# S5's preparation on S5's own pages, layer 0's column tiles in a new order, retention in nine turns

## The chip, the core and the metric

One core of one Trainium2 chip runs the whole program. The metric is the device time in microseconds; the median of three runs of the kernel before is 1762.29 us (1761.71 to 1763.96).

## What is computed

Two layers of a hybrid network on 640 tokens (128 of a context pass, 512 of a denoising step), 1024 features each, all in 32-bit floats. Per layer, cut to what matters here:

```python
mod = silu(cond) @ mod_w + mod_b                 # six vectors sh1, sc1, g1, sh2, sc2, g2
h = rmsnorm(x, norm1_w) * (1 + sc1) + sh1
proj = h @ w_in                                  # 1024 -> 2568 columns
pa, pb, pc, pd = split(proj)                     # SSD, retention, S5, LRU
ya = ssd_mixer(pa);  yb = retention_mixer(pb)
yc = s5_mixer(pc);   yd = lru_mixer(pd)
x = x + g1 * (concat(ya, yb, yc, yd) @ w_out)
h = rmsnorm(x, norm2_w) * (1 + sc2) + sh2
x = x + g2 * conv_ffn(h)
```

SSD and retention are chunked scans with 128-token chunks, S5 is a complex diagonal scan, LRU a real one; each runs in both directions. S5 needs tables (powers and angles of its decay, products of its input and output matrices) that depend on the parameters alone; the kernel computes them too.

## The kernel before

Features lie on partitions, the 640 tokens along the free dimension, in two halves of 320. A matrix product in 32 bits is made of three products in a rounded format: weights and activations are split into a high and a low part (`hi`, `lo`, `hhi`, `hlo`), and `mm3` multiplies high by high, high by low and low by high. `wsplit` (line 186) fetches 512 columns of weights into `raw`, rounds them on ScalarE into `hi`, and subtracts on GpSimd and VectorE in turn into `lo`. `col_tile` (line 214) makes one column tile: 128 output features from all 1024 inputs, 48 matmuls of 320 columns, into two of the three PSUM banks of tag `mm`.

Working memory is given out in pages of 128 x 648 floats under tags: A, B and C have 12 each, Ya, Yb, Yc and Yd two each, H 16 (line 121). A tile takes a free page of its tag, and a helper adds an order between first writes: of two tiles of one tag, the one that comes first in the program is first written first. So a tile waits for a free page and for all earlier tiles of its tag to have been begun. Banks are given out in the same way (line 124: `mm` three, `b` two, `a`, `c` and `mod` one each). The order on each engine is laid down when the program is built, by a planner that takes the program's order as priority and its own estimates of durations; on the chip every engine works through its list in order. DMAs are all issued from the SP queue.

In the layer (line 1360) each mixer is a generator, and the string `ORDER` (line 44) says whose next turn is emitted. The mixers' column tiles are made in their turns: two for S5, two for LRU, two for LRU's gate (`gb`), one narrow one and four for SSD, two for its gate (`z`), and for retention two each for queries and keys (q0, k0, q1, k1), two for the gate (g0, g1) and the values (v). The turn "a0" or "a1" is the attention over one pair of heads. After every turn in layer 0 two rounds of the modulation product are emitted (`filler`, line 321): a round fetches two pages of `mod_w` (`mraw`, on the two pages of Yd) and makes 8 small matmuls; `drain` emits what is left, ahead of the first turn that needs Yd for retention's output.

In layer 0, S5's preparation (`s5_prep`, line 592) is emitted just behind S5's column tiles. Its tiles are under three tags, set by `ST = 'AAC'`: powers, angle tables and small matrices on A (12 pages, those LRU and retention use as well), the four large turns on C (those of SSD). Its PSUM tiles are on the one bank `c`. In layer 1 the preparation is made during the feed-forward part of layer 0, and all on C. S5's scans, and the eight tiles of `x` themselves, are on B: `x` is freed when it has been normalized, and fetched again (`load_x`, line 177) behind S5's last tile; the residual of the output projection needs it.

The output projection is in two halves: LRU and S5 (8 tiles), then SSD and retention. Its inputs are split onto pages (`yhi`, `ylo`; `parts`, line 1407); the first half takes the pages of tag H, on which the normalized activations were.

Of the kernel before, what the change touches and what calls it, by code (L numbers as in the profile page):

```python
# [12 lines left out]
AF = mybir.ActivationFunctionType  # L13
# [16 lines left out]
NF = 22  # L30
TB = 81
SK = 2
PB = "c"
EXTRA = ''
TBA = 1
PCP = 1
# [2 lines left out]
TSR = 1  # L39
LB = 1  # L40
FPS = 2
ST = 'AAC'
MR = 'C'

ORDER = ("s5 gb lru lru gb ssd ssd z lru ssd z ret ret ssd ret ssd ret ret ret ret",
         "s5 ssd gb lru ssd lru gb z lru ssd z ret ssd ret ret ssd ret ret ret ret")
RAWS = 5
SPLITS = 5

# [26 lines left out]
def hybrid_kernel(ctx: ExitStack, tc: tile.TileContext, I, O, dbg=None):  # L76
# [3 lines left out]
    sec = ["start"]  # L80
# [45 lines left out]
    def page(tag, dt=F32, name="pg"):  # L126
        t = pgp.tile([P, PGB if tag == "B" else PGW], dt, tag=tag, name=name, bufs=PAGES[tag])
        fresh[t.tensor.name] = tag
        return t

    def paged(tag, shape, name, dt=F32):
        n = int(np.prod(shape))
        t = page(tag, dt, name)[:, :n]
        if len(shape) == 1:
            return t
        names = "abcd"[:len(shape)]
        return t.rearrange(f"p ({' '.join(names)}) -> p {' '.join(names)}", **dict(zip(names[1:], shape[1:])))

    def bank(tag):
        t = psp.tile([P, 512], F32, tag=tag, name=tag, bufs=BANKS[tag])  # L140
        fresh[t.tensor.name] = tag
        return t
# [43 lines left out]
    def wsplit(ap, n, cut=512, le=None, tag=None):  # L186

        out = []
        for c0 in range(0, n, cut):
            w = min(cut, n - c0)  # L190
            raw = wp.tile([P, 512], F32, tag="raw", name="raw", bufs=RAWS)
            SP.dma_start(raw[:, :w], ap[:, c0:c0 + w])
            if tag:
                hi, lo = page(tag, F32R, "whi")[:, :512], page(tag, F32R, "wlo")[:, :512]
            else:
                hi = wp.tile([P, 512], F32R, tag="hi", name="hi", bufs=SPLITS)
                lo = wp.tile([P, 512], F32R, tag="lo", name="lo", bufs=SPLITS)
            A.copy(hi[:, :w], raw[:, :w])
            lo_i[0] += 1
            (le or lo_eng[lo_i[0] % len(lo_eng)]).tensor_tensor(lo[:, :w], raw[:, :w], r2f(hi[:, :w]), op=ALU.subtract)  # L200
            out.append((c0, c0 + w, hi, lo))
        return out
# [289 lines left out]
    M_, A_, S_ = ALU.mult, ALU.add, ALU.subtract  # L492
# [99 lines left out]
    def s5_prep(l):  # L592

        wb, wc, tb, zz = s5d[l]
        p1, p2, p3 = "CCC" if l else ST

        def keep(name, shape):
            return smp.tile([P] + shape, F32, tag=f"k_{name}", name=name)
# [65 lines left out]
            G.tensor_copy(s5x0[l][DH[d], :, :, d].rearrange("p g i -> p i g"), x0[DH[d]])  # L664
        yield


        ek = [u8]
        for k in range(1, 6):
# [4 lines left out]
        for q in range(2):  # L674
            o = 8 * q
# [43 lines left out]
             [bb[:, i] for i in range(2)], [bt[:, i] for i in range(2)])  # L719
        ncq = paged(p2, [16, 16], "ncq")  # L720
        V.tensor_scalar(ncq, cq[:, 1], -1.0, None, op0=M_)
        cm = [paged(p2, [16, 32], f"cm{i}") for i in range(2)]
        for i, c in enumerate((cq[:, 0], ncq)):
            G.memset(cm[i], 0.0)
            for d in range(2):
# [65 lines left out]
    def s5_mixer(l, hh, y, steps):  # L791
# [132 lines left out]
        for i in range(2):  # L924
            tp = page("B", name="glut")
            for h in range(2):
                o, n = HALF[h]
                t = tp[:, o:o + n]
                for vg in (1, 0):
                    ps = bank("b")  # L930
                    for k in range(2):
                        m = 256 * vg + 128 * i
                        T.matmul(ps[:, :n], gw[k][:, m:m + 128], yt[k][:, o:o + n], start=k == 0, stop=k == 1)
                    if vg:
                        A.activation(t, ps[:, :n], AF.Tanh, scale=0.5)
                    else:
                        V.scalar_tensor_tensor(t, t, 1.0, ps[:, :n], op0=A_, op1=M_)
                G.tensor_scalar(y[i][:, o:o + n], t, 0.5, None, op0=M_)


    def lru_mixer(l, hh, y):
# [296 lines left out]
    def ret_mixer(l, hh, y):  # L1238
# [9 lines left out]
        def rotated(u):  # L1248
            pss = col_tile(wsplit(I["w_in"][l, u], 1024), hh)
            q = page("A", name="rq")  # L1250
            evac(pss, q)
            sw = page("A", name="rsw")
            V.stream_shuffle(sw[:, :512], q[:, 128:640], swap)
            V.tensor_tensor(sw[:, :512], sw[:, :512], sinp[:, :512], op=M_)
            G.tensor_tensor(q[:, 128:640], q[:, 128:640], cosp[:, :512], op=M_)
            V.tensor_tensor(q[:, 128:640], q[:, 128:640], sw[:, :512], op=A_)
            return q
# [35 lines left out]
                            T.matmul(out, S[d][:, k - 1], qe[d][:, k - 1], start=False, stop=d == 1)  # L1293
                A.copy(y[t][:, 128 * k0:128 * (k0 + n)], ps[:, 0:128 * n])

        yield
        q = rotated(12)
        yield
        kx = rotated(13)
        yield  # L1300
        units = wsplit(I["w_in"][l, 14], 1024) + wsplit(I["w_in"][l, 15], 1024)
        vk = [paged("B", [5, 128], "rv") for _ in range(2)]
        for c0 in (0, 2, 4):
            n = min(2, 5 - c0)
            ps = bank("b")
            old = sec[0]
            sec[0] = old + "*"
            for c in range(n):
                for k in range(8):
                    hi, lo = units[k // 2][2:]  # L1310
                    w = slice((k % 2) * 256, (k % 2) * 256 + 256)

                    mh, ml = [v[:, 128 * (c0 + c):128 * (c0 + c) + 128] for v in hh[k]]
                    o = ps[:, 256 * c:256 * c + 256]
                    T.matmul(o, mh, hi[:, w], start=k == 0, stop=False)
                    T.matmul(o, mh, lo[:, w], start=False, stop=False)
                    T.matmul(o, ml, hi[:, w], start=False, stop=k == 7)
            sec[0] = old
            for i in range(2):
                A.copy(vk[i][:, c0:c0 + n], ps[:, 0:256 * n].rearrange("p (c w) -> p c w", w=256)[:, :, 128 * i:128 * i + 128])  # L1320
        attend(0, q, kx)
        yield
        q = rotated(16)
        yield
        kx = rotated(17)
        gg = [page("A", name="rg") for _ in range(2)]
        gt = gates(l, hh, (18, 19), gg, None if TSR else AF.Silu)
        next(gt)
        for _ in range(2):
            yield  # L1330
            next(gt)
        attend(1, q, kx)
        SP.dma_start(O["st_ret"][l], so)

        nw = smp.tile([P, 2], F32, tag="rnw", name="rnw")
# [24 lines left out]
    def layer(l, norm):  # L1360
# [6 lines left out]
            for h in HO:  # L1367
                norm.apply(l, 0, h, hh, ks)
        normed = hold[1]
        ys = {n: [page(tag, name="y" + n) for _ in range(2)] for n, tag in (("lru", "Ya"), ("ssd", "Yb"), ("s5", "Yc"))}  # L1370
        ys["ret"] = []
        gens = {"s5": s5_mixer(l, hh, ys["s5"], steps), "lru": lru_mixer(l, hh, ys["lru"]), "ssd": ssd_mixer(l, hh, ys["ssd"]),
                "ret": ret_mixer(l, hh, ys["ret"]), "gb": gates(l, hh, (2, 3), ys["lru"], AF.Gelu_apprx_tanh),
                "z": gates(l, hh, (9, 11), ys["ssd"], None if TSZ else AF.Silu)}
# [10 lines left out]
                hold[0] = None  # L1385
        order = ORDER[l].split()
        for i, n in enumerate(order):
            if n == "ret" and "ret" not in order[:i]:
                if l == 0:
                    drain()  # L1390
                ys["ret"] += [page("Yd", name="yret") for _ in range(2)]
                step(n + str(l), gens[n])
            step(n + str(l), gens[n])
            if i == 0 and l == 0:
                load_x(0)
            if l == 0 and i >= 1:
                filler(FPS)
# [346 lines left out]
```

## Time and profile before

| | us |
|---|---|
| median of three runs | 1762.29 |
| the profiled execution | 1760.15 |
| its span, first to last instruction | 1758.30 |
| TensorE matmul busy | 1659.0 |
| VectorE busy | 1042.9 |
| ScalarE busy | 712.0 |
| GpSimd busy | 466.2 |

The profile is of one execution. Engines are named PE (TensorE), PEld (its weight loads, which overlap), DVE (VectorE), ACT (ScalarE), POOL (GpSimd) and SP (the queue that issues DMAs). Almost every instruction is recorded under line 92, a helper, so that groups are told apart by the names of their tiles: `out<-in`. Matmuls overlap, so that the busy time of a group can be longer than the stretch it ran in.

### The profile page before, as it was taken

How to read it: one execution, taken by the hardware profiler on the slowest of the kernel's cores; microseconds unless marked ns; L12 is line 12 of the kernel's file. 1: busy time of each engine (PE TensorE's matmuls, PEld its weight loads, DVE VectorE, ACT ScalarE, POOL GpSimd, SP SyncE). 2: the span in 40 equal slices, each digit the busy share in tenths (PEclk: the TensorE clock that was granted, in tenths of full speed). 3: DMA queues.
4: the chain of work that ended last, by engine and by line, in shares of the span. 5: the costliest groups of instructions: out<-in, count | busy, mean ns of one | idle time of the engine just before them, and what ended most of it. 6: DMA issues, size and time to landing. Idle time of an engine off the chain costs nothing.

```text
span 1758.3 us, 30749 instructions
## 1 busy us (share of the span) xinstructions
PE 1659.0 (94%) x11342; PEld 1532.9 (87%) x11342; DVE 1042.9 (59%) x2482; ACT 712.0 (40%) x1566; POOL 466.2 (27%) x652
## 2 busy tenths in 40 slices
PE   7877999999999999999988999899999999999997
PEld 3655787888999999999988889798889999999996
DVE  7776976977433773455367678588753343334345
ACT  5724534645321343332335364555453233233244
POOL 2221343413211211221223244432332111211222
PEclk9977999999999999999999999999999999999998
DMA  9465564321435445543333334422112222222321
GB/s 323 148 203 144 176 204 135 90 75 49 125 124 164 152 159 182 184 144 114 97 94 129 113 103 135 144 76 75 37 60 61 79 84 64 88 76 60 94 73 61
DMA packets 143433, 206.50 MB, mean 117 GB/s; under 512 B 22852, under 2 KB 64692, under 8 KB 143284
## 3 DMA queue, kind: packets, MB, share of 16 engines
q1 hardware_dynamic: 143284, 204.54, 37.3%
q8 instruction: 90, 1.47, 0.3%
q14 instruction: 59, 0.48, 0.1%
HBM read 184.42 MB, written 20.07 MB: 116 GB/s over the span
## 4 chain that ended last, share of the span: by engine, by line
PE 77%; DVE 10%; DMA 4%; ACT 3%; issue 3%; POOL 2%; SPq 0%; DVEq 0%; POOLq 0%; ACTq 0%
PE mm L92 65%; PE b L92 6%; PE mod L92 4%; PE c L92 2%; DMA mraw<-in_mod_w 1%; DVE nt L92 1%; DVE x L92 1%; DVE s5r L92 1%; PE a L92 1%; DVE lo L92 1%; POOL lo L92 1%; DVE nsq L92 1%; DMA wb<-wb 1%; ACT hhi L92 1%; DVE sE L92 1%
## 5 line engine op out<-in xcount | busy, mean ns | idle before, releaser
L92 PE MATMUL mm<-hhi,hi 128*128 128x320 f32 x1976 | 624.0, 317 | 17.1 <-ACT hhi L92 11.1
L92 PE MATMUL mm<-hlo,hi 128*128 128x320 f32 x1976 | 622.5, 315 | 5.5 <-POOL hlo L92 2.9
L92 PE MATMUL mm<-hhi,lo 128*128 128x320 f32 x1976 | 617.6, 314 | 0.3 <-DVE lo L92 0.3
L92 ACT CAST hi<-raw 128x512 fp32r<-128x512 f32 (+1 forms) x384 | 227.2, 593 | 594.6 <-PE mm L92 358.5
L92 POOL TENSOR_TENSOR lo<-raw,hi 128x512 fp32r<-128x512 f32 (+1 forms) x200 | 258.0, 1291 | 675.1 <-ACT hi L92 615.3
L92 PEld LDWEIGHTS mm<-hhi,hi 128*128 128x128 f32 x1976 | 375.3, 190 | 37.1 <-ACT hhi L92 16.0
L92 PEld LDWEIGHTS mm<-hlo,hi 128*128 128x128 f32 x1976 | 375.3, 190 | 15.4 <-POOL hlo L92 5.5
L92 PEld LDWEIGHTS mm<-hhi,lo 128*128 128x128 f32 x1976 | 374.9, 190 | 4.3 <-issue 2.2
L92 DVE TENSOR_TENSOR lo<-raw,hi 128x512 fp32r<-128x512 f32 (+1 forms) x184 | 127.3, 692 | 210.3 <-ACT hi L92 202.4
L92 DVE SCALAR_TENSOR_TENSOR x<-mm,mod,x 128x320 f32<-128x320 f32 (+2 forms) x288 | 117.4, 435 | 208.5 <-PE mm L92 206.9
L92 PE MATMUL mm<-fal,hi 128*128 128x320 f32 x640 | 197.4, 309 | 0.0
L92 PE MATMUL mm<-fah,lo 128*128 128x320 f32 x640 | 197.3, 309 | 0.0
L92 PE MATMUL mm<-fah,hi 128*128 128x320 f32 x640 | 195.2, 311 | 0.2 <-DVE x L92 0.2
L92 PEld LDWEIGHTS mm<-fah,hi 128*128 128x128 f32 x640 | 119.2, 188 | 5.4 <-issue 2.5
L92 PEld LDWEIGHTS mm<-fah,lo 128*128 128x128 f32 x640 | 120.4, 188 | 0.4 <-issue 0.4
L92 PEld LDWEIGHTS mm<-fal,hi 128*128 128x128 f32 x640 | 120.4, 188 | 0.0
L92 DVE TENSOR_TENSOR fa<-fc,mm 128x128 f32<-128x128 f32 x132 | 45.2, 373 | 98.1 <-PE mm L92 92.5
L92 PE MATMUL mod<-mraw,s 128*32 128x256 f32 x768 | 69.2, 415 | 18.7 <-DMA mraw<-in_mod_w 18.1
L92 DVE SCALAR_TENSOR_TENSOR fc<-fraw,par,fc 128x643 f32<-128x643 f32 x88 | 81.1, 923 | 2.8
L92 PE MATMUL mm<-yhi,hi 128*128 128x320 f32 x192 | 60.6, 317 | 1.6 <-DVE rg L92 1.1
L92 PE MATMUL mm<-ylo,hi 128*128 128x320 f32 x192 | 60.8, 317 | 1.2 <-DVE ylo L92 1.2
L92 PE MATMUL mm<-yhi,lo 128*128 128x320 f32 x192 | 61.1, 318 | 0.0
(350 smaller groups left out, 2425.7 us busy)
## 6 DMA issues: line engine op xcount, KB each, us to landing
raw<-in_up SPq DMA_DIRECT2D x176, 256.0 KB
mraw<-in_mod_w SPq DMA_DIRECT2D x160, 256.0 KB
raw<-in_w_in SPq DMA_DIRECT2D x80, 256.0 KB
raw<-in_dn SPq DMA_DIRECT2D x96, 192.0 KB
mraw<-in_mod SPq DMA_DIRECT2D x32, 256.0 KB
raw<-in_w_o SPq DMA_DIRECT2D x32, 256.0 KB
tb<-tb SPq DMA_DIRECT2D x16, 326.0 KB
x<-in_x SPq DMA_DIRECT2D x16, 320.0 KB
```

Source lines behind the costliest of these rows:

```text
L92: r = f(*a, **k)
```

## The change

- S5's preparation in layer 0 keeps A only for its powers (`pw`, `pwt`, `apcw`, `pz`). Angle tables, matrices and large turns are on B, the pages of S5 itself; two tiles (`cm`) are on C. Its PSUM tiles are on the two banks `b`.
- The order of layer 0 is a new one: LRU's first tile ahead of its gate, SSD's three in a row, and retention's values early.
- Retention is cut into named parts, and `RET` says for each layer which part comes in which turn. In layer 0 these are nine turns (values, q0, k0, both gates, first attention, q1, k1, second attention), in layer 1 the seven that there were. The values are under tag Yc instead of B and on the banks `mm` instead of `b`. The pages of retention's output are taken, and the modulation product is drained, ahead of the turn of the first attention instead of ahead of retention's first turn.
- S5's output stays in the page on B in which it was made; the scaling by one half is done in place, and the two pages of Yc that it had are those of the values.

```diff
-PB = "c"
+PB = "b"
-ST = 'AAC'
-ORDER = ("s5 gb lru lru gb ssd ssd z lru ssd z ret ret ssd ret ssd ret ret ret ret",
+ORDER = ("s5 lru gb lru ssd ssd ssd z ret gb z lru ret ret ssd ret ssd ret ret ret ret ret",
          "s5 ssd gb lru ssd lru gb z lru ssd z ret ssd ret ret ssd ret ret ret ret")
+RET = (("v", "q0", "k0", "g0", "g1", "a0", "q1", "k1", "a1"),
+       ("q0", "k0", "v a0", "q1", "k1", "g0", "g1 a1"))
...
-        p1, p2, p3 = "CCC" if l else ST
+        p1, p2, p3, pc = ("C", "C", "C", "C") if l else ("A", "B", "B", "C")
...
+        p1 = p2
...
-        cm = [paged(p2, [16, 32], f"cm{i}") for i in range(2)]
+        cm = [paged(pc, [16, 32], f"cm{i}") for i in range(2)]
...
-                G.tensor_scalar(y[i][:, o:o + n], t, 0.5, None, op0=M_)
+                G.tensor_scalar(t, t, 0.5, None, op0=M_)
+            y.append(tp)
...
+            vk[:] = [paged("Yc", [5, 128], "rv") for _ in range(2)]
+                ps = bank("mm")
...
+        def part(n):
+            if n in "q0 k0 q1 k1":
+                qk[n] = rotated({"q0": 12, "k0": 13, "q1": 16, "k1": 17}[n])
+            elif n == "v":
+                values()
+            elif n in "a0 a1":
+                attend(int(n[1]), qk.pop("q" + n[1]), qk.pop("k" + n[1]))
+            else:
+                if not gg:
+                    gg[:] = [page("A", name="rg") for _ in range(2)]
+                    part.g = gates(l, hh, (18, 19), gg, None if TSR else AF.Silu)
+                    next(part.g)
+                next(part.g)
+
+        for turn in RET[l]:
             yield
-            next(gt)
-        attend(1, q, kx)
+            for n in turn.split():
+                part(n)
...
-        ys = {n: [page(tag, name="y" + n) for _ in range(2)] for n, tag in (("lru", "Ya"), ("ssd", "Yb"), ("s5", "Yc"))}
-        ys["ret"] = []
+        ys = {n: [page(tag, name="y" + n) for _ in range(2)] for n, tag in (("lru", "Ya"), ("ssd", "Yb"))}
+        ys["s5"], ys["ret"] = [], []
...
-            if n == "ret" and "ret" not in order[:i]:
+            if n == "ret" and "a0" in RET[l][order[:i].count("ret")]:
                 if l == 0:
                     drain()
                 ys["ret"] += [page("Yd", name="yret") for _ in range(2)]
+            if n == "ret" and "ret" not in order[:i]:
                 step(n + str(l), gens[n])
```

## Rows read from the trace of the kernel before

**Rows 1.** The page: span, TensorE's busy time, its granted clock in 40 slices

```profile
span 1758.3 us, 30749 instructions
...
PE 1659.0 (94%) x11342; PEld 1532.9 (87%) x11342; DVE 1042.9 (59%) x2482; ACT 712.0 (40%) x1566; POOL 466.2 (27%) x652
...
PEclk9977999999999999999999999999999999999998
```

**Rows 2.** Busy time by stretch: PE, PEld, DVE, ACT, POOL, granted clock, DMA share, GB/s

```profile
84.60:160.40 75.80, 49.33 (x321) 32.07 (x321) 47.71 (x85) 27.43 (x61) 11.25 (x25) 0.68 0.63 192
160.40:394.00 233.60, 221.42 (x1541) 194.83 (x1540) 188.85 (x420) 113.59 (x265) 83.54 (x116) 1.00 0.44 134
76.60:394.00 317.40, 278.75 (x1917) 234.09 (x1916) 243.11 (x531) 148.81 (x348) 96.24 (x142) 0.92 0.49 150
980.00:1241.50 261.50, 247.25 (x1675) 227.53 (x1673) 201.97 (x438) 134.73 (x300) 96.52 (x132) 0.99 0.34 105
```

**Rows 3.** Tiles in 0 to 480 us: count, ns, first and last start

```profile
L92 ACT COPY lraw<-mm x6: 253/334/457, 102.5 to 158.2; 128x128 f32<-128x128 f32 x2, 128x192 f32<-128x192 f32 x2, 128x320 f32<-128x320 f32 x2
L92 SPq DMA_DIRECT2D lgw<-in_lgw x2: 423/423/423, 104.1 to 104.5; - x2
L92 ACT COPY kk<-c x4: 257/266/287, 102.4 to 152.8; 128x128 f32<-128x128 f32 x4
L92 ACT COPY dtc<-mm x2: 399/404/410, 152.9 to 162.9; 16x320 f32<-16x320 f32 x2
```

**Rows 4.** Timeline of PE: start, us, what, idle before and releaser

```profile
91.45 1.08 PE L92 MATMUL mod<-mraw,s 128*32 128x256 f32 x8 [6.80 <-DMA mraw<-in_mod_w]
...
144.21 1.08 PE L92 MATMUL mod<-mraw,s 128*32 128x256 f32 x8 [3.72 <-DMA mraw<-in_mod_w]
```

**Rows 5.** Groups of PE, 84.6 to 160.4 us, then 160.4 to 394 us

```profile
L92 PE MATMUL mod<-mraw,s 128*32 128x256 f32 x80 | 9.9, 584 | 18.1 <-DMA mraw<-in_mod_w 18.1
...
L92 PE MATMUL mod<-mraw,s 128*32 128x256 f32 x88 | 8.9, 391 | 0.0
```

**Rows 6.** DVE, 60 to 76.6 us: groups of the tables; timeline

```profile
L92 DVE TENSOR_TENSOR tab<-tab,tabt 128x8 f32<-128x8 f32 (+5 forms) x17 | 3.3, 214 | 0.0
L92 DVE TENSOR_TENSOR tabt<-tab,e 128x16 f32<-128x16 f32 (+4 forms) x14 | 3.2, 228 | 0.0
L92 DVE TENSOR_TENSOR tab<-tab,e 128x16 f32<-128x16 f32 (+4 forms) x14 | 3.1, 224 | 0.0
...
60.50 0.33 DVE L92 MEMSET amask<- 128x328 f32 x1
...
76.60 0.77 DVE L92 STREAM_TRANSPOSE s5u<-b 128x256 f32<-128x256 f32 x2
```

**Rows 7.** Tiles in 0 to 480 us: preparation's large turns, S5's output

```profile
L92 DVE TENSOR_TENSOR pmr<-pmr,pt x8: 678/680/684, 92.2 to 143.0; 128x512 f32<-128x512 f32 x8
...
L92 DVE SCALAR_TENSOR_TENSOR glut<-glut,b x4: 486/487/489, 268.2 to 276.2; 128x320 f32<-128x320 f32 x4
```

**Rows 8.** Tiles in 0 to 480 us: residual, x, retention's rotations and output

```profile
L92 DVE SCALAR_TENSOR_TENSOR x<-mm,mod,x x48: 335/408/552, 345.5 to 424.3; 128x128 f32<-128x128 f32 x16, 128x192 f32<-128x192 f32 x16, 128x320 f32<-128x320 f32 x16
L92 SPq DMA_DIRECT2D x<-in_x x16: 327/430/610, 2.1 to 275.7; - x16
...
L92 ACT COPY rq<-mm x8: 399/426/433, 220.9 to 317.9; 128x320 f32<-128x320 f32 x8
L92 DVE TENSOR_TENSOR rq<-rq,rsw x4: 680/690/693, 227.2 to 325.0; 128x512 f32<-128x512 f32 x4
...
L92 ACT CAST yhi<-yret x2: 724/728/732, 387.8 to 393.0; 128x640 fp32r<-128x640 f32 x2
```

**Rows 9.** Timelines: a convolution step alone, one beside GpSimd, that GpSimd instruction

```profile
246.25 0.84 DVE L92 SCALAR_TENSOR_TENSOR sxc<-sraw,par,sxc 128x643 f32<-128x643 f32 x1
...
301.40 1.91 DVE L92 SCALAR_TENSOR_TENSOR sxc<-sraw,par,sxc 128x643 f32<-128x643 f32 x1
...
300.88 1.74 POOL L92 TENSOR_TENSOR lo<-raw,hi 128x512 fp32r<-128x512 f32 x1
```

More of the change, by code (lines that the diff above doesn't have):

```diff
@@ L1294, in attend @@
                 A.copy(y[t][:, 128 * k0:128 * (k0 + n)], ps[:, 0:128 * n])
[L1296 to L1327, printed above, removed]
-        next(gt)
-        for _ in range(2):
+        vk, qk, gg = [], {}, []
+        def values():
+            units = wsplit(I["w_in"][l, 14], 1024) + wsplit(I["w_in"][l, 15], 1024)
+            vk[:] = [paged("Yc", [5, 128], "rv") for _ in range(2)]
+            for c0 in (0, 2, 4):
+                n = min(2, 5 - c0)
+                ps = bank("mm")
+                old = sec[0]
+                sec[0] = old + "*"
+                for c in range(n):
+                    for k in range(8):
+                        hi, lo = units[k // 2][2:]
+                        w = slice((k % 2) * 256, (k % 2) * 256 + 256)
+                        mh, ml = [v[:, 128 * (c0 + c):128 * (c0 + c) + 128] for v in hh[k]]
+                        o = ps[:, 256 * c:256 * c + 256]
+                        T.matmul(o, mh, hi[:, w], start=k == 0, stop=False)
+                        T.matmul(o, mh, lo[:, w], start=False, stop=False)
+                        T.matmul(o, ml, hi[:, w], start=False, stop=k == 7)
+                sec[0] = old
+                for i in range(2):
+                    A.copy(vk[i][:, c0:c0 + n], ps[:, 0:256 * n].rearrange("p (c w) -> p c w", w=256)[:, :, 128 * i:128 * i + 128])
@@ L1330, in ret_mixer @@
+        for turn in RET[l]:
             yield
-            next(gt)
-        attend(1, q, kx)
+            for n in turn.split():
+                part(n)
         SP.dma_start(O["st_ret"][l], so)
```

## The prediction

> **What bounds the kernel now.** I read the page first. TensorE is busy for nearly the whole span, so a change to the order of the work pays only where TensorE idles or is slow, and the row of slices shows where: the granted clock is full almost everywhere but in the first tenth of the span [rows 1]. Next I read busy time by stretch [rows 2]. From 84.60 to 160.40 us TensorE is busy for 49.33 of 75.80 us, at a mean granted clock of 0.68, a mix of the levels 1.2 and 2.4 GHz. From there to 394.00 it is busy for 221.42 of 233.60 us (94.8%) at full clock. So what there is to win in layer 0 lies in 76 us.
>
> The tile view says why TensorE has nothing to do there [rows 3]. The page of LRU's first tile (`lraw`) is written by ScalarE from 102.5 us on, that of its second up to 158.2 us, and LRU's gate weights (`lgw`) are fetched only at 104.1 us: they all take tag A, behind every page that S5's preparation takes there, and preparation's last product (`kk`) is written at 152.8 us. The page of SSD's step sizes (`dtc`) is first written at 152.9 us: tag C, behind preparation's large tiles. With three `mm` banks in order, a tile that cannot be emptied stops all later column tiles. What is left for TensorE is modulation matmuls, and these wait for their weights: at 91.45 us after 6.80 us of idleness, at 144.21 us after 3.72 [rows 4]. In the stretch 80 of them cost 9.9 us and 18.1 us of waiting, at 584 ns each; in the stretch behind it 88 cost 8.9 us, at 391 ns, with no wait [rows 5].
>
> **The change part by part.**
>
> *Pages of preparation and the order of layer 0.* Preparation keeps on A only its powers; one of those four pages (`apcw`) lives to its end, so LRU has 11 of 12, and one tile takes 10. SSD's pages come behind two of preparation (`cm`) instead of all its large ones. The column tiles of LRU, both gates, SSD and retention's values can then run on from 84.60 us. Busy time at a clock of 0.68 holds about (1 - 0.68) x 49.33 = 15.8 us of slowness [rows 2]; idle time counts in that clock too, so I take 14, and the work of the stretch is 49.33 - 14 = 35.3 us. At the density of the next stretch, 0.948, it fills 37.3 us. TensorE alone would therefore be done 75.8 - 37.3 = **38.5 us** earlier. That is the ceiling.
>
> *VectorE.* It becomes the second bound. From 76.60 to 394.00 us it has 243.11 us of work [rows 2]. The preparation's angle tables move into this time: they begin at 60.50 us now, on tag A, but on B they are ordered behind S5's input pages, the last of which is written from 76.60 us on. Their three large groups before 76.6 us are 3.3 + 3.2 + 3.1 = 9.6 us [rows 6]. Between 0 (something else is moved forward into the hole) and 9.6 I take the whole, since the first LRU tile comes only behind S5's tiles: 252.7 us. TensorE's work in the same time is 278.75 - 14 = 264.8, together 517.5 us for both engines. In the dense stretch the two together were busy (221.42 + 188.85) / 233.60 = 1.756 of the time, in layer 1's mixers, where no preparation is in the way, (247.25 + 201.97) / 261.50 = 1.718 [rows 2]. The work then takes 294.7 or 301.2 us instead of 317.4: a gain of 22.7 or 16.2 us. I take the middle, **19.4 us**.
>
> *Six pages instead of twelve in preparation's loop.* On B, S5's two inputs, `bb`, `cq`, `ncq` and `kk` stay; six pages rotate for eleven uses in each of four turns. A turn has 12 operations on VectorE of 680 ns, 8.2 us, and the last end at 143 us now [rows 7]. Bounds: 53 us for the loop as now, or 33 if only VectorE counts, so between no change and some 20 us earlier for S5, less the 14 us by which the tables start later. S5's last tile is made until 276.2 us [rows 7], x is fetched again behind it until 275.7, and its first residual is at 345.5 us [rows 8]: 69 us of room. Whatever becomes of S5 inside that costs nothing; if it were later than that, the output projection would wait. The first two scans, which now run beside preparation, come behind it; they are in the same room.
>
> *Retention in nine turns.* Values go through `mm` banks and tag Yc, the gate tiles come before the first attention, and q1 and k1 come last. The same matmuls, evictions and DMAs are issued. What is new is behind the last column tile: now it is a gate, which needs no rotation; then it is k1. From the last eviction of `rq` at 317.9 to the end of its last rotation at 325.0 + 0.7 us are 7.8 us [rows 8]. The first half of the output projection covers that if TensorE still has it to do, so the cost is 0 to 7.8; I take **3 us**, nearer to the covered end, because 8 projection tiles stand there. SP's order changes with it: weights of gates and values are asked for earlier, the modulation weights by two rounds a step as before. The seven turns of layer 1, its values on other banks and pages, and S5's output scaled in place add no instruction; TensorE lost 14.3 of 261.50 us in layer 1's mixers [rows 2], and for banks I allow 3 us to either side and take 0.
>
> **Sum.** 19.4 - 3 = 16.4 us less than the profiled execution's own 1760.15 us (span 1758.3): 1743.7. That execution was 2.1 us under the median of the three runs, 1762.29, so I say **1746 us**; the sum's own range, with all of 22.7 or with 7.8 paid and 16.2 won, is 1735 to 1757 with the 3 us of layer 1.
>
> **The rivals.**
>
> *TensorE alone decides.* VectorE gives way, its waits being on TensorE's tiles. For it: in the stretch 84.60 to 160.40 VectorE itself is idle for 28 of 76 us [rows 2]. Against it: to end 38.5 us earlier VectorE would have to be busy for 252.7 of 278.9 us, 91%, and no long stretch shows more than 81%. Time: 1762.3 - 38.5 + 0 to 3, 1724 to 1727; with what lies up to the forecast's range, 1724 to 1735. Chance 0.13.
>
> *VectorE sets the end, and nothing is gained.* At the dense stretch's own filling, 188.85 / 233.60 = 0.808, its 252.7 us take 312.7, 4.7 less than now, and the tail of 3 to 7.8 us eats that: 1761 to 1765, and with what lies up to the forecast 1757 to 1766. For it: operations of VectorE get longer where GpSimd works beside them: the same convolution step took 0.84 us at 246.25 and 1.91 us at 301.40, while a split on GpSimd lasted from 300.88 for 1.74 us [rows 9]. Packing weight splits closer brings more such meetings. This is the rule in the Trainium skill, SBUF — State Buffer, section Who interferes with whom: the two engines share a pair of ports, and who has it locks the other out for a whole instruction. The trace agrees, 1.91 against 0.84 us; by that rule alone every split moved beside a two-input operation costs VectorE up to that difference, and the gain would be nearer to this rival than to mine. Against it: the filling of 0.808 was reached with TensorE at 95%, so it is a floor. Chance 0.13.
>
> *Slower: the modulation matmuls hold up the column tiles.* They stand in TensorE's order at places laid down before the run. Now their waits stop little else; with column tiles behind them each wait counts. The 18.1 us of waits are seven, 2.6 us each [rows 5]. There are 21 rounds of 8 from 84.60 us on [rows 5]; if each waited 2.6 us, that were 54 us. TensorE's 264.8 us at 0.948 are 279.3, with 54 us 333 instead of 317.4: 16 us slower, 1778. It decides from a mean wait of 38.5 / 21 = 1.8 us a round. For it: two pages a round, so no round is fetched ahead. Against it: the 11 rounds that stood between column tiles had no wait at all [rows 5]. S5 later by over 69 us would end the same way. Chance 0.15, from just above 1766 to 1778.
>
> That the change doesn't do what it says is the second rival's time: if the second LRU tile still waited for a page, the column tiles would stop as before.
>
> **How the numbers follow.** Forecast 0.59, TensorE alone 0.13, no gain 0.13, slower 0.15. About 0.2%, 3.5 us, is what a measurement of this kernel can tell from no change: below 1758.8 is faster, above 1765.8 slower. All of the forecast and of the first rival and a little of the second are faster, 0.74; most of the second is the same, 0.11; the rest, 0.15, slower. The range of 8 in 10 leaves out the lower half of the first rival and the upper half of the last: 1728 to 1769.
>
> **What would show it.** Right: in 84 to 160 us a granted clock near 1 and TensorE busy over 90%; `lgw` fetched and `lraw`, `dtc` evicted before 110 us; the 18.1 us of modulation waits down to a few; the last `yhi` of retention, which begins at 393.0 us now [rows 8], some 16 us earlier, and everything behind it shifted by as much. VectorE's share up to that point should rise from 77% to about 84%. Step by step: angle tables starting after 74 us and S5's output before 300 us. Wrong: `lraw` of the second tile still after 140 us; waits for modulation weights of over 1.8 us a round; x fetched after 340 us; a gap of over 8 us between the output projection's first half and the second; or a shift in layer 1 larger than 3 us.

## The result and the profile after

The changed kernel takes **1785.53 us** (median of 4 runs, 1784.13 to 1788.62) against 1762.31 for the kernel before beside it: a ratio of 1.0133, interval 1.0115 to 1.0150. It is 23 us slower where 16 us less had been forecast, and outside the range of 1728 to 1769.

The page of the changed kernel: span, busy time, TensorE's clock in 40 slices.

```profile
span 1786.7 us, 30738 instructions
...
PE 1679.7 (94%) x11342; PEld 1554.5 (87%) x11342; DVE 1040.4 (58%) x2482; ACT 717.1 (40%) x1570; POOL 476.3 (27%) x652
...
PEclk9989987799999999999999999999999999999998
```

The dip of the clock in the third and fourth slice of [rows 1] is all but gone, and another has come in the seventh and eighth (268 to 357 us). Busy time by stretch of the changed kernel, with the columns of [rows 2]:

```profile
84.60:160.40 75.80, 67.85 (x488) 55.01 (x486) 60.40 (x154) 48.15 (x110) 18.82 (x26) 0.93 0.53 166
160.40:260.00 99.60, 90.96 (x635) 79.48 (x633) 70.50 (x129) 41.33 (x93) 36.77 (x54) 0.94 0.63 188
260.00:360.00 100.00, 75.97 (x409) 62.40 (x409) 70.74 (x188) 43.02 (x111) 30.09 (x44) 0.76 0.33 107
```

and the last of these stretches in the kernel before:

```profile
260.00:360.00 100.00, 93.31 (x654) 82.24 (x654) 78.20 (x181) 55.38 (x146) 40.48 (x43) 1.00 0.37 110
```

In 84.60 to 160.40 us TensorE now makes 488 matmuls at a clock of 0.93, against 321 at 0.68 [rows 2]: what the change is for, it does. From 260 to 360 us it makes 409 where it made 654. The early gain is lost there, and more. The tiles that answer to [rows 3], changed kernel:

```profile
L94 ACT COPY lraw<-mm x6: 257/339/452, 68.8 to 123.9; 128x128 f32<-128x128 f32 x2, 128x192 f32<-128x192 f32 x2, 128x320 f32<-128x320 f32 x2
L94 SPq DMA_DIRECT2D lgw<-in_lgw x2: 328/328/328, 25.7 to 27.8; - x2
L94 ACT COPY kk<-b x4: 266/266/268, 120.0 to 189.6; 128x128 f32<-128x128 f32 x4
L94 ACT COPY dtc<-mm x2: 397/406/414, 97.3 to 103.8; 16x320 f32<-16x320 f32 x2
```

LRU's and SSD's tiles come 34 and 56 us earlier than in [rows 3], but preparation's last `kk` comes 37 us later. The tiles that answer to [rows 6 to 8], with the first attention's `ktok`:

```profile
L94 DVE MEMSET amask<- x2: 65/198/332, 73.9 to 75.5; 128x328 f32 x1, 128x8 f32 x1
L94 DVE TENSOR_TENSOR pmr<-pmr,pt x8: 660/684/687, 106.8 to 193.4; 128x512 f32<-128x512 f32 x8
L94 PE MATMUL b<-s5u,wb x80: 231/275/503, 209.2 to 313.1; 128*128 128x81 f32 x80
L94 DVE SCALAR_TENSOR_TENSOR glut<-glut,b x4: 477/483/489, 329.8 to 340.2; 128x320 f32<-128x320 f32 x4
L94 ACT COPY ktok<-b x4: 256/420/585, 339.7 to 373.4; 128x128 f32<-128x128 f32 x2, 128x512 f32<-128x512 f32 x2
L94 SPq DMA_DIRECT2D x<-in_x x8: 328/382/425, 321.9 to 339.1; - x8
L94 DVE SCALAR_TENSOR_TENSOR x<-mm,mod,x x48: 336/406/552, 374.2 to 451.0; 128x128 f32<-128x128 f32 x16, 128x192 f32<-128x192 f32 x16, 128x320 f32<-128x320 f32 x16
L94 ACT CAST yhi<-yret x2: 724/726/727, 414.3 to 419.3; 128x640 fp32r<-128x640 f32 x2
```

S5's output is made till 340.2 us, 64 us later than in [rows 7]; `ktok` begins at 339.7; retention's last `yhi` at 419.3, **26.3 us later** than 393.0 [rows 8]. From there to the same point of layer 1 (1240.7 before, 1266.1 after) are 847.7 and 846.8 us: 26.3 of the 28.4 us by which the two profiled spans differ are there when layer 0's mixers end. Below, "the end of the mixers" is the start of that last `yhi`.

Why `ktok` starts with S5's end is seen in TensorE's timeline of the changed kernel:

```profile
292.02 0.57 PE L94 MATMUL b<-s5r,wc 128*128 128x81 f32 x4
...
298.23 2.08 PE L94 MATMUL c<-sxs,btok 128*128 128x128 f32 x8
305.16 1.14 PE L94 MATMUL b<-s5r,wc 128*128 128x81 f32 x4 [4.85 <-DMA wc<-wc]
...
337.97 1.24 PE L94 MATMUL b<-s5y,glu 128*128 128x320 f32 x4
339.05 0.27 PE L94 MATMUL b<-ct,rq 128*128 128x128 f32 x1
```

and of the kernel before:

```profile
274.84 1.34 PE L92 MATMUL b<-s5y,glu 128*128 128x320 f32 x4
275.78 0.52 PE L92 MATMUL b<-hi,hhi 128*128 128x256 f32 x1
...
293.22 0.27 PE L92 MATMUL b<-ct,rq 128*128 128x128 f32 x1
```

The first attention matmul (`ct,rq`) follows S5's last (`s5y,glu`) within 1.1 us. Both are on the banks `b`, of which there are two, given out in program order. In the kernel before, the values (`hi,hhi` and so on) stood between them on the same banks, for 17 us. The order, S5 and then the attention, was the same; S5 was only early enough. In the changed kernel the column tiles are used up at 292 us. From there to 296 us TensorE is busy for 2.34 of 4 us, and from 296 to 310 us its granted clock is 0.50, already ahead of the 4.85 us of waiting for `wc`: four matmuls take 0.57 us at 292.02, at the upper level of 2.4 GHz, and 1.14 us at 305.16, at the lower of 1.2.

### The profile page after: what moved, and what is told of

Its sections match the earlier page's. It is cut to its first block, busy times and chain, and to the rows that moved or that the text cites. A ratio compares the mean times of both kernels' runs of the same rounds, so it can differ in the third digit from the quotient of the medians.

```text
span 1786.7 us, 30738 instructions
## 1 busy us (share of the span) xinstructions
PE 1679.7 (94%) x11342; PEld 1554.5 (87%) x11342; DVE 1040.4 (58%) x2482; ACT 717.1 (40%) x1570; POOL 476.3 (27%) x652
## 4 chain that ended last, share of the span: by engine, by line
PE 74%; DVE 12%; DMA 5%; ACT 3%; issue 3%; POOL 2%; SPq 1%; DVEq 0%; POOLq 0%; ACTq 0%
PE mm L94 63%; PE b L94 5%; PE mod L94 3%; DMA mraw<-in_mod_w 1%; PE c L94 1%; DVE x L94 1%; DVE nt L94 1%; SPq L94 1%; DVE sE L94 1%; PE a L94 1%; POOL lo L94 1%; DVE s5r L94 1%; DVE nsq L94 1%; DVE lo L94 1%; DMA raw<-in_dn 1%
## 5 line engine op out<-in xcount | busy, mean ns | idle before, releaser
L94 POOL TENSOR_TENSOR lo<-raw,hi 128x512 fp32r<-128x512 f32 (+1 forms) x200 | 263.1, 1316 | 703.8 <-ACT hi L94 645.1
L94 PE MATMUL mod<-mraw,s 128*32 128x256 f32 x768 | 64.4, 394 | 9.5 <-DMA mraw<-in_mod_w 8.4
```

Of the source, the lines that this page charges most:

```text
L94: r = f(*a, **k)
```

## The experiments

The theory: the pages alone delay S5, and S5 delays the attention through the banks `b`. Rivals: the new order or the nine turns cost the time; or only one of pages and banks matters. All runs, times in us; `kk`, S5's output (`glut`) and the end of the mixers are the starts of the last instruction, `ktok` that of the first, all from one profiled execution each, which lies up to 5 us off its kernel's median; ratios are to the kernel before on the same chip (1761.09 to 1764.00 us):

| kernel | median | ratio, interval | `kk` | `glut` | `ktok` | end of the mixers |
|---|---|---|---|---|---|---|
| before | 1762.31 | | 152.8 | 276.2 | 296.1 | 393.0 |
| changed | 1785.53 | 1.0115 to 1.0150 | 189.6 | 340.2 | 339.7 | 419.3 |
| E1 pages only | 1783.48 | 1.0094 to 1.0133 | 180.4 | 328.1 | 327.6 | 414.4 |
| E2 order only | 1772.72 | 1.0038 to 1.0068 | 146.2 | 278.8 | 295.9 | 402.4 |
| E3 matrices on C | 1759.81 | 0.9974 to 1.0001 | 166.1 | 307.0 | 306.8 | 387.9 |
| E4 attention off `b` | 1762.17 | 0.9979 to 1.0012 | 189.8 | 353.2 | 274.1 | 388.0 |
| E5 both | 1751.72 | 0.9918 to 0.9965 | 165.4 | 327.7 | 257.4 | 380.7 |
| E6 both, tables on A | 1748.96 | 0.9903 to 0.9949 | 146.8 | 293.0 | 260.4 | 377.2 |
| E7 E5, old order | 1749.83 | 0.9908 to 0.9955 | 174.3 | 320.3 | 251.2 | 384.2 |
| E8 E2, attention off `b` | 1769.21 | 1.0018 to 1.0056 | 144.6 | 274.4 | 292.3 | 397.9 |
| E9 before, attention off `b` | 1781.69 | 1.0096 to 1.0137 | 151.4 | 275.2 | 258.4 | 404.0 |
| E10 E6, old order | 1749.83 | 0.9919 to 0.9944 | 143.1 | 297.7 | 261.1 | 382.6 |
| E11 changed, tables on A | 1776.46 | 1.0066 to 1.0097 | 163.2 | 316.0 | 314.3 | 407.4 |
| E12 E2, SSD earlier | 1762.43 | 0.9985 to 1.0008 | 144.1 | 280.3 | 305.3 | 395.8 |
| E13 E6, SSD earlier | 1756.86 | 0.9953 to 0.9976 | 146.5 | 300.8 | 275.6 | 390.1 |
| E14 changed, bank `c` | 1795.73 | 1.0166 to 1.0207 | 203.2 | 348.5 | 348.0 | 425.3 |
| E15 E6, bank `c` | 1766.74 | 1.0004 to 1.0029 | 158.0 | 329.9 | 256.9 | 398.0 |

**E1, the pages alone.** Old order and old turns in layer 0, everything else as changed.

```diff
-ORDER = ("s5 lru gb lru ssd ssd ssd z ret gb z lru ret ret ssd ret ssd ret ret ret ret ret",
+ORDER = ("s5 gb lru lru gb ssd ssd z lru ssd z ret ret ssd ret ssd ret ret ret ret",
-RET = (("v", "q0", "k0", "g0", "g1", "a0", "q1", "k1", "a1"),
+RET = (("q0", "k0", "v a0", "q1", "k1", "g0", "g1 a1"),
```

> The new pages with the turns of layer 0 in the old order (values with the first attention, gates behind k1). Theory (preparation is starved by its six rotating pages on B, S5 ends some 60 us late, and retention's attention stands behind S5 in the order of the banks b): the last product kk is written after 170 us, S5's output ends after 300 us, time 1775 to 1800. Rival (the early column tiles bring VectorE work of LRU and SSD that delays preparation, pages do not matter): kk before 160 us, S5's output before 285 us, time within 6 us of the 1762 of before.

```profile
L94 ACT COPY kk<-b x4: 256/266/267, 119.4 to 180.4; 128x128 f32<-128x128 f32 x4
L94 DVE SCALAR_TENSOR_TENSOR glut<-glut,b x4: 477/482/487, 317.7 to 328.1; 128x320 f32<-128x320 f32 x4
```

1783.48 us, 2 us under the changed kernel: the pages make it slow. (E1 keeps the banks `b` of preparation and the new places of the values, too; without those banks it is slower still, E14.) The pages also do all that fills the early stretch: from 84.60 to 160.40 us TensorE is busy for 68.22 us at 0.95 here, 67.85 at 0.93 with the new order.

**E2, the order alone.** Pages and bank of preparation as before.

```diff
-PB = "b"
+PB = "c"
-        p1, p2, p3, pc = ("C", "C", "C", "C") if l else ("A", "B", "B", "C")
+        p1, p2, p3, pc = ("C", "C", "C", "C") if l else ("A", "A", "C", "A")
```

> The new order of turns with the old pages of preparation (powers, tables and matrices on A, large turns on C, bank c). Theory: preparation is as quick as before (kk before 165 us, S5's output before 290 us), the column tiles wait for its pages again (second LRU tile emptied after 140 us), time 1755 to 1772. Rival (the order alone is what is slow): kk after 175 us or S5's output after 310 us, time above 1780.

1772.72 us, 10 us slower than before and 0.7 us above the theory's range. S5 is as early as before, and so is `ktok`; here SSD is late (E12). With E1's 21 us the parts add up to 31; together they cost 23.

**E3, preparation's matrices on C.** Layer 0's matrices and inputs (`p2`) move to C, the tables stay on B: ten pages of B rotate in the loop instead of six.

```diff
-        p1, p2, p3, pc = ("C", "C", "C", "C") if l else ("A", "B", "B", "C")
+        p1, p2, p3, pc = ("C", "C", "C", "C") if l else ("A", "C", "B", "C")
...
-        p1 = p2
+        p1 = "C" if l else "B"
```

> The changed kernel with preparation's small matrices (bq, cq, bb, bt, ncq, kk, with cm) on C instead of B, so that ten pages of B rotate in the loop instead of six. Theory: the loop from the first pmr to the last kk shrinks from 85 us to 45 to 65, S5's output ends 20 to 40 us before its 340 us, time 1755 to 1775. Rival (VectorE and TensorE, not pages, are what the loop waits for): loop within 8 us of 85, time within 6 us of 1785.

Tile view of E3:

```profile
L94 DVE TENSOR_TENSOR pmr<-pmr,pt x8: 659/682/899, 101.2 to 169.1; 128x512 f32<-128x512 f32 x8
L94 DVE SCALAR_TENSOR_TENSOR glut<-glut,b x4: 470/480/489, 298.2 to 307.0; 128x320 f32<-128x320 f32 x4
L94 ACT COPY ktok<-b x4: 265/416/579, 306.8 to 346.0; 128x128 f32<-128x128 f32 x2, 128x512 f32<-128x512 f32 x2
```

and its busy time by stretch:

```profile
260.00:360.00 100.00, 87.85 (x542) 74.79 (x541) 81.33 (x203) 51.57 (x130) 39.51 (x46) 0.90 0.42 128
```

The loop's products now span 67.9 us instead of 86.6 (50.8 in [rows 7]), a little more than the 45 to 65 expected, S5 is 33 us earlier, and so is `ktok`, 0.2 us before S5's last output. The time falls by 26 us, to that of the kernel before. That the loop is still longer than before has a cause that the page counts don't hold: VectorE works on other mixers' tiles between its steps, as the changed kernel's timeline shows in the second turn:

```profile
125.20 0.68 DVE L94 TENSOR_TENSOR pmi<-bb,apcw 128x512 f32<-128x512 f32 x1
127.27 0.83 DVE L94 SCALAR_TENSOR_TENSOR lT<-lg,lT 128x644 f32<-128x644 f32 x1 [1.39 <-ACT lT L94]
128.02 0.88 DVE L94 SCALAR_TENSOR_TENSOR sxc<-sraw,par,sxc 128x643 f32<-128x643 f32 x1
128.82 0.82 DVE L94 SCALAR_TENSOR_TENSOR lT<-lg,lT 128x644 f32<-128x644 f32 x1
129.56 0.68 DVE L94 TENSOR_TENSOR pt<-bb,apcw 128x512 f32<-128x512 f32 x1
...
135.77 1.77 DVE L94 TENSOR_TENSOR pmi<-pmi,pt 128x512 f32<-128x512 f32 x1
```

The first and the last step of one product lie 10.6 us apart. LRU's and SSD's work (`lT`, `sxc`), which stood behind preparation before, now stands within it. From the start of the first to the end of the last `pmr<-pmr,pt`, VectorE is busy for 40.05 of 51.5 us in the kernel before, for 67.11 of 87.3 in the changed kernel and for 61.93 of 68.6 in E3. So four pages more take its idle time in the loop from 20 to 7 us, and what is left of the lengthening is other mixers' work.

**E4, the attention on other banks.** Pages as changed; in layer 0 the attention takes `mod` and `mm`.

```diff
+            b1, b2 = ("mod", "mm") if l == 0 else ("b", "b")
-            tokens(kx, lambda k: 128 * k, "b", lambda ps, k0, n: A.copy(ktok[:, k0:k0 + n], ps))
+            tokens(kx, lambda k: 128 * k, b1, lambda ps, k0, n: A.copy(ktok[:, k0:k0 + n], ps))
...
-            S = enter_states("A", "b", I["st_ret"][l], t, ktok, vs, lambda d, k: rcd[:, d, t:t + 1], so[:, :, t])
+            S = enter_states("A", b1, I["st_ret"][l], t, ktok, vs, lambda d, k: rcd[:, d, t:t + 1], so[:, :, t])
...
-                pss = [bank("b") for _ in range(2)]
+                pss = [bank(b) for b in (b1, b2)]
...
-                ps = bank("b")
+                ps = bank(b1)
```

> The changed kernel with the attentions of layer 0 on the banks mod and mm instead of b, so that they do not stand behind S5's scans in the order of the banks b. Theory: the first ktok is written before 300 us instead of at 339, the output of retention ends 10 to 30 us before its 420 us, time 1758 to 1777, S5's output as late as in the changed kernel (330 to 350). Rival (the attention waits for SSD, pages of A or VectorE): ktok after 325 us, time within 4 us of 1785.

Tile view of E4:

```profile
L94 DVE SCALAR_TENSOR_TENSOR glut<-glut,b x4: 474/482/489, 339.0 to 353.2; 128x320 f32<-128x320 f32 x4
L94 ACT COPY ktok<-mod x4: 265/450/585, 274.1 to 340.1; 128x128 f32<-128x128 f32 x2, 128x512 f32<-128x512 f32 x2
...
L94 ACT CAST yhi<-yret x2: 727/728/729, 379.6 to 388.0; 128x640 fp32r<-128x640 f32 x2
```

S5 is even later than in the changed kernel (3 us past the range expected), the attention starts 66 us earlier, and the mixers end 31 us earlier: the changed kernel's loss is the attention behind a late S5. No gain on the kernel before is left, though. S5 is 77 us later here than there, more than the 69 us of room to the residual, whose first start is at 363.1 us (333.3 in E6); that this takes the gain is likely and was not tested by itself.

**E5, both.** The diffs of E3 and E4 together; their cores:

```diff
+        p1, p2, p3, pc = ("C", "C", "C", "C") if l else ("A", "C", "B", "C")
+            b1, b2 = ("mod", "mm") if l == 0 else ("b", "b")
```

> The changed kernel with both edits: S5's matrices on pages C (ten pages rotate, the tables alone on B) and layer 0's attention on the banks mod and mm. Theory (two separate delays of the changed kernel: preparation short of pages, and the attention standing behind S5 in the order of the banks b; each edit takes one away, so together they gain more than either): last page pair written near 166 us, S5's output near 300 to 310 us, ktok from 265 to 285 us, last yhi<-yret of layer 0 between 368 and 382 us against 393.0 before, time 1740 to 1755 us. Rival (once the attention or S5's output is early, TensorE's and VectorE's work up to the first FFN holds the end whatever comes first): last yhi<-yret at 386 to 390 us as in either edit alone, time 1757 to 1764 us.

1751.72 us, faster than the kernel before and than either edit alone: two separate delays, as the theory has it. S5's output came later than expected (327.7 us) and the attention earlier (257.4); with the attention ahead, that no longer decides.

**E6, the tables back on A.** E5 with

```diff
-        p1 = "C" if l else "B"
+        p1 = "C" if l else "A"
```

> The kernel with both edits, and S5's tables on pages A, where they stood before the change, in place of B. Theory (the tables start 14 us later on B only because they follow the second set of S5's own pages or the mixers' first evictions in VectorE's order, and what counts is how many pages the matrices rotate): tables' start within 4 us of the kernel with both edits, time within 5 us of it. Rival (the tables' pages set when preparation starts): tables from 60 to 65 us, pmr<-bb first at 85 to 92 us, S5's output 10 to 14 us earlier, time 5 to 12 us less. A third way: the pages A are then held by the tables when the LRU wants them, and the projections slow down: lraw's last eviction 10 us or more later, time 5 to 15 us more.

Tile view of E6:

```profile
L94 DVE MEMSET amask<- x2: 65/198/332, 61.3 to 61.7; 128x328 f32 x1, 128x8 f32 x1
L94 DVE TENSOR_TENSOR pmr<-pmr,pt x8: 680/684/693, 80.3 to 153.9; 128x512 f32<-128x512 f32 x8
L94 DVE SCALAR_TENSOR_TENSOR glut<-glut,b x4: 483/489/489, 276.5 to 293.0; 128x320 f32<-128x320 f32 x4
L94 ACT CAST yhi<-yret x2: 727/727/727, 368.4 to 377.2; 128x640 fp32r<-128x640 f32 x2
```

and its stretch that answers to the third of [rows 2]:

```profile
76.60:394.00 317.40, 291.40 (x2012) 249.97 (x2011) 244.85 (x559) 159.24 (x365) 97.79 (x143) 0.96 0.49 150
```

The tables were held back by the pages of B: on A they start 14 us earlier, and S5 ends 35 us earlier than in E5. That is the rival's mechanism, and more of it than it said, but the time is the theory's: 2.8 us less, with overlapping intervals. S5 no longer sets the end. This is the lowest median of all, 13 us under the kernel before.

**E7 and E10, the old order in E5 and in E6.** Both with E1's two lines.

```diff
-ORDER = ("s5 lru gb lru ssd ssd ssd z ret gb z lru ret ret ssd ret ssd ret ret ret ret ret",
+ORDER = ("s5 gb lru lru gb ssd ssd z lru ssd z ret ret ssd ret ssd ret ret ret ret",
```

> The kernel with both edits, but layer 0's order of column tiles and retention's turns as before the change. Theory (the new order is worth its time only where preparation and the attention do not stand in the way; then it fills TensorE early): slower than the kernel with both edits by 5 to 15 us, 1750 to 1765 us. Rival (the gain of the two edits comes from pages and banks alone, the order is worth nothing): within 3 us of the kernel with both edits.

> The fastest kernel so far (matrices on C, tables on A, attention on mod and mm; 1748.96 us) with layer 0's order of column tiles and retention's turns as before the change. Theory (with preparation and attention out of the way, pages and banks make the gain and the order of the tiles none): within 5 us of 1748.96, last yhi<-yret within 6 us of 377.2. Rival (with the tables on A the projections wait for those pages again, lraw's last eviction is at 131.4 us against 111.3, and the new order is what fills TensorE meanwhile): 1755 to 1765 us.

1749.83 us twice, against 1751.72 and 1748.96. In E7 the theory's 5 to 15 us did not come, its rival did; E10 confirmed it. The mixers end 3.5 and 5.4 us later with the old order, but the new order and the nine turns are worth no time that these runs can tell.

**E8 and E9, the banks where preparation is as before.** E4's diff in E2 and in the kernel before.

```diff
+            b1, b2 = ("mod", "mm") if l == 0 else ("b", "b")
```

> The new order and turns with S5's pages as before the change (as in the run of the order alone, 1772.72 us) and layer 0's attention on the banks mod and mm. Theory (in that kernel SSD is the late one, its product at 383.6 us, not the attention, which starts at 295.9 us as before): ktok from 255 to 285 us, but last yhi<-yret within 6 us of 402.4 and time 1766 to 1774 us. Rival (the attention holds it there too): last yhi<-yret at 375 to 390 us, time 1745 to 1760 us.

> The kernel before, whole, with only layer 0's attention on the banks mod and mm. Theory (in the kernel before S5 ends at 276.2 us and the attention starts at 296.1 us, so it waits for S5 by little; the banks are worth time only where S5 is late): ktok from 280 to 296 us, last yhi<-yret within 5 us of 393.0, time 1757 to 1768 us. Rival (the attention's place in the order of the banks b costs the kernel before too, and the gain of the kernel with both edits is mostly this): last yhi<-yret at 375 to 386 us, time 1745 to 1756 us.

E8 went as the theory has it in time and end, though `ktok` came later than expected. E9 fits neither: 20 us slower. In E9's tile view the attention begins 38 us earlier, but its values are still those of the banks `b`, and it ends later:

```profile
L92 ACT COPY ktok<-mod x4: 254/418/573, 258.4 to 353.8; 128x128 f32<-128x128 f32 x2, 128x512 f32<-128x512 f32 x2
...
L92 ACT COPY rv<-b x6: 254/361/381, 281.9 to 292.9; 128x256 f32<-128x256 f32 x4, 128x128 f32<-128x128 f32 x2
...
L92 ACT CAST yhi<-yret x2: 727/730/732, 395.2 to 404.0; 128x640 fp32r<-128x640 f32 x2
```

So moving off `b` is no gain in itself; it pays where S5 is late and the values are ready. Of the 20 us, 11 are lost in layer 0; the rest builds up behind it, and its cause stays open, as does what in the sharing of `mm` costs the 11.

**E11, the tables alone.** The changed kernel with E6's line in place of `p1 = p2`.

```diff
-        p1 = p2
+        p1 = "C" if l else "A"
```

> The changed kernel with the tables alone back on pages A; the matrices stay on the six pages of B, the attention on the banks b. Theory (both the later start and the six pages make preparation late): tables from 61 us, pmr<-bb first at 76 to 90 us, but the loop, from there to the last kk, still 75 to 90 us long; last kk from 160 to 175 us, S5's output from 310 to 325 us, last yhi<-yret from 395 to 408 us, time 1763 to 1776 us. Rival (the tables on B are what holds the pages of the matrices, and with them gone the loop is as short as on C): loop 50 to 65 us, last kk by 150 us, S5's output by 300 us, time under 1762 us.

1776.46 us, half a microsecond above the theory's range; everything else lies in it: from the first `pmr` at 82.2 to the last `kk` at 163.2 us the loop takes 81 us, although it starts 22 us earlier. The six pages hold it, not the tables.

**E12 and E13, SSD's second half earlier.** The same line in E2 and in E6.

```diff
-ORDER = ("s5 lru gb lru ssd ssd ssd z ret gb z lru ret ret ssd ret ssd ret ret ret ret ret",
+ORDER = ("s5 lru gb lru ssd ssd ssd z ret gb z lru ssd ret ret ssd ret ret ret ret ret ret",
```

> The order alone (S5's pages as before the change), with SSD's fourth turn moved ahead of retention's q0 and k0 and its fifth behind k0. Theory (the new order puts retention's value tiles between SSD's third and fourth turn, so SSD's second half starts 25 us later than before the change, 284.9 against 259.2 us for its first exponent, and ends the mixers): first sE from 250 to 262 us, yhi<-yssd from 355 to 375 us, last yhi<-yret from 390 to 396 us, time 1758 to 1767 us. Rival (the order costs its time elsewhere, retention's products being pushed behind one another): SSD earlier by as much, last yhi<-yret still from 399 to 405 us, time 1769 to 1776 us.

> The same move of SSD's turns in the kernel with matrices on C, tables on A and attention on mod and mm (1748.96 us), where yhi<-yssd ends at 358.7 us and the last yhi<-yret at 377.2 us. Theory (SSD is no longer the last there, retention is): yhi<-yssd from 335 to 350 us, last yhi<-yret within 5 us of 377.2, time within 4 us of 1748.96. Rival (TensorE idles from 260 to 360 us, 88.42 of 100 us busy, for want of work that SSD's late second half holds back): last yhi<-yret from 364 to 372 us, time 1736 to 1744 us.

Tile views of E2 and, below the dots, E12:

```profile
L94 ACT ACTIVATE sE<-ct,dt x20: 384/388/404, 284.9 to 374.5; 128x128 f32<-128x128 f32 x20
L94 ACT CAST yhi<-yssd x2: 720/722/725, 397.6 to 398.3; 128x640 fp32r<-128x640 f32 x2
```

```profile
L94 ACT ACTIVATE sE<-ct,dt x20: 384/387/404, 260.7 to 337.8; 128x128 f32<-128x128 f32 x20
L94 ACT CAST yhi<-yssd x2: 720/723/726, 369.9 to 370.5; 128x640 fp32r<-128x640 f32 x2
```

SSD's first exponent (`sE`) comes 24 us earlier, its output 28, and the 10 us that the order cost are gone: it had put SSD's fourth turn behind retention's values, q0 and k0. In E13 both accounts fail: SSD is earlier as expected (344.3 us), but the attention starts 15 us later and the kernel is 8 us slower. There retention is the late one, and what is moved ahead of it is paid for.

**E14 and E15, the bank alone.** Preparation's products on `c` again, in the changed kernel and in E6.

```diff
-PB = "b"
+PB = "c"
```

> The changed kernel with preparation's products on the one bank c again, as before the change; pages, order and turns as changed. Theory (S5's scans come behind preparation by the order of the pages B, which its large turns and the scans share, not by the banks): first scan still after the last kk, at 200 us or later, S5's output after 325 us, last yhi<-yret from 410 to 425 us, time 1778 to 1795 us. Rival (the scans stand behind preparation in the order of the banks b): first scan from 105 to 150 us, beside preparation as in the kernel before, S5's output before 310 us, time 1755 to 1770 us.

> The same in the kernel with matrices on C, tables on A and attention on mod and mm (1748.96 us; first scan at 163.0 us, S5's output till 293.0 us). Theory (banks are not what orders the scans, and one bank for the transposes in place of two makes preparation's loop longer by a few us, in room that S5 has there): last kk from 146 to 160 us, first scan from 160 to 180 us, time within 5 us of 1748.96. Rival (the bank c belongs to SSD, whose products now stand behind preparation's): SSD's first exponent 10 us or more later than 238 to 242 us, time 1755 to 1770 us.

In both the scans still come behind the last `kk` (from 220.0 and 175.1 us): not the banks put them there. The pages do. E2 differs from E14 in preparation's pages alone, with the large turns on C instead of B, and its first scan is 113 us earlier, beside preparation:

```profile
L94 PE MATMUL b<-s5u,wb x80: 231/275/365, 106.9 to 244.6; 128*128 128x81 f32 x80
...
L94 PE MATMUL b<-s5u,wb x80: 231/275/500, 220.0 to 318.7; 128*128 128x81 f32 x80
```

E8 and E15 have the tables on A and keep the matrices off B, and differ in the large turns in the same way: 105.2 against 175.1 us. So it is the large turns on the scans' own pages. E14 is 10 us slower than the changed kernel, just over the range. In E15 the loop's 12 us, of which the theory said that S5 had room for them, cost 18, near the rival's price, but not by its early sign: `sE` begins at 248.1 us against 246.6 in E6 (the 238 to 242 of the text is another kernel's) and ends 8 us later. S5 is not what costs it: in E5 its output is as late (327.7 against 329.9 us) at 1751.72 us, while SSD's output in E15 comes 14 us later than in E6 (373.0 against 358.7). So the two banks `b` are a good part of the change, 10 us in the changed kernel and 18 in E6.

## Why the prediction was wrong

**The step that failed** is "Whatever becomes of S5 inside that costs nothing", with its 69 us of room. S5 came 64 us later (37 of them at preparation's last `kk`, 27 behind it, where the scans now stand), so inside, and x was fetched till 339.1 us, just short of the 340 named as the sign of failure; yet 26 us were lost. The room was counted to the residual, which needs x. Nearer was the attention, next behind S5 on the banks `b`, and there the room was the 17 us of the values that the change itself took out from between. 64 - 17 = 47 us is about what `ktok` lost (43.6). E4 shows it: with S5 just as late and the attention elsewhere, the mixers end 31 us earlier. For a gain there was no room at all on those banks: in E6 the attention begins at 260.4 us, before S5's old end of 276.2 [rows 7].

**The loop on six pages** was bounded by 33 and 53 us. It took 86.6 by the row that answers to [rows 7], and 67.9 with ten pages (E3): the prediction named the six pages and put their shortage at nothing, and it measures 18.7 us. The rest is in the upper bound "as now", which took for granted that VectorE would still do the loop nearly alone; it works through the mixers that the same change brings forward. The tables began at 73.9 us, as foreseen, but S5's output came at 340.2 us and not before 300.

**The early stretch** was right in kind: TensorE busy for 67.85 of 75.80 us (89.5%, just short of the 90 of the list), `lgw` and `dtc` before 110 us, `lraw` a little after. It was the pages, though, not the order (E1).

**The size** was right where nothing takes it back: E6 ends the mixers 15.8 us earlier than the kernel before, against "some 16 us", at 1748.96 us against 1746. Up to the end of its mixers (76.6 to 378 us) VectorE is busy for 237.01 of 301.40 us, 79%, and not the 84% foreseen, while TensorE rises from 88% to 91%. E6 is another kernel, and E7 and E10 reach the same time with the old order, so the agreement is in part luck and does not prove the sum that led there. The sum's own range is also uneven: 1735 is counted from 1760.15, 1757 from 1762.29.

**Retention's tail** of 3 us could not be told apart: E7 and E10 put the old turns back and change nothing that shows. **Layer 1** was right (847.7 against 846.8 us).

**The rivals.** The modulation waits from 60 to 420 us fell from 18.1 to 7.9 us, so the rival that ended slower had the sign but not the cause; its last sentence, on S5, named the cause and asked for 69 us where 17 decide. TensorE alone and VectorE as the bound were not put to the test. By the Trainium skill, SBUF — State Buffer, section Who interferes with whom, a VectorE instruction with two inputs in SBUF contends with a GpSimd instruction that reads SBUF. The trace agrees in single steps: the `pmi` step shown at 135.77 us took 1.77 us beside a split on GpSimd (135.12 us, for 1.88), against 0.68 elsewhere. In the sum the closer packing did not lengthen VectorE's work: it is busy for 1040.4 us in all, 1042.9 before [rows 1].

## What to carry to other kernels

When a step moves later, look for its room in every order that it stands in, banks and pages too, and take the nearest user behind it; the consumer of its data can be the farther one. When a change takes work out from between two users of one buffer, it takes away room as well. And a loop's time "as now" holds only while the engines that it needs are not given the work that the change brings forward.
